# Seven products for eight in a 256-token block of an output projection, and reciprocal roots that start on ScalarE

## The chip, the cores and the metric

The kernel runs on one core of a Trainium2 chip, as one launch. The metric is the device time of that launch in microseconds (us), before and after the change. A core has five engines with queues of their own, each of which works in order: PE (TensorE, the matmuls), DVE (VectorE), ACT (ScalarE), POOL (GpSimd) and SP (SyncE, which here only starts transfers). They wait for one another by semaphores. PE's results go to PSUM, from which DVE and ACT read them; everything else lies in SBUF or, for inputs, outputs and scratch, in DRAM.

## The reference

One decoder layer on 4096 tokens of width 1024, in float32. All three mixers (a gated MLP over chunks, a gated linear recurrence, a forgetting attention) read the same normed and projected input; what they give is concatenated to `y`, and one output projection adds it to `x`. A last norm closes. The part that matters here:

```python
def _rmsnorm(x, g):
    xf = x.astype(jnp.float32)
    y = xf * lax.rsqrt(jnp.mean(xf * xf, axis=-1, keepdims=True) + NORM_EPS)
    return (y * g.astype(jnp.float32)).astype(x.dtype)
...
        y = jnp.concatenate([y_a, y_b, y_c], axis=-1)
        x = x + jnp.einsum('bse,ed->bsd', y, w_out[layer])
    return _rmsnorm(x, final_norm_g)
```

`w_out` is 1024 x 1024, so the last product is 4096 x 1024 x 1024.

## The kernel before

The kernel has three stages one after the other: the input projection with the first two mixers (to about 1620 us), the attention (1651 to 3031), and the output projection (from 3031.3 to the end). Float32 products are made of three PE passes: each operand is split into a high part, rounded to the type that PE multiplies fast (`hi`), and the rest (`lo`), and hi·hi + hi·lo + lo·hi is summed in PSUM. The split of an operand is one ACT copy (the rounding) and one DVE subtraction.

The output projection takes 32 tiles of 128 tokens (`out_tile`), two of which make a block of 256 tokens with index t. For a block, `y_load` brings `y` (transposed) from DRAM scratch in two tiles `yr0` and `yr1`, by five transfers, and `y_split` splits them into `yhi` and `ylo`, in tiles of 128x1024. `w_out` was loaded and split during the attention by `load_wo`, into eight pairs `wo_hi`, `wo_lo` of 128x1024, one for each 128 rows. For a tile, each of the two column halves is one PSUM tile `o` of 24 matmuls (8 row groups times three passes) of 128 x 128 by 128 x 512 (L1588), so 96 matmuls a block. DVE adds the PSUM half to `x` (L1592), ACT squares the sum and adds it up along the row (L1594); then the second half of the generator, run while the next tile multiplies, adds both halves' sums (L1596), takes the reciprocal root in `rsqrt_small` (L99 to L106: a first guess from the bits and three Newton steps, eleven small DVE operations with the two around them), scales the tile with it and with the norm's weights `fgB` (L1600), and writes it out (L1601).

`x` comes into tiles named `x3` (the profile drops the digit: `x`), which rotate over four buffers `qb0` to `qb3` that the attention used for its queries. PE's order is that of the program text (it is scheduled by hand); the order on the other engines is set at build time by the framework's scheduler, and is fixed when the program runs. A pool's buffer is given out in turn: a tile that takes a buffer over waits until the last reader of the tile before has ended, and a load into it until an output transfer from it has landed.

`rsqrt_small` serves other norms too: the one at the start for the first tokens' `x` (names `xr0`, `xr1`), one for the other tokens' (`xr`), and two within the mixers (`gr`, `or`).

## Time and profile before

| what | us |
|---|---|
| three runs, median (lowest to highest) | 3394.76 (3393.18 to 3395.24) |
| the profiled execution | 3389.97 |
| its span | 3388.1 |
| first matmul of the output projection starts | 3031.3 |
| last matmul of the output projection starts | 3379.4 |

The mean clock granted to PE was 0.985 of full speed. Busy times over the whole span: PE 3264.9 us (96%), DVE 2337.5 (69%), ACT 1615.7 (48%), POOL 1383.7 (41%). In the output projection POOL does next to nothing: 3.00 us in 348. In a row of a group or line the columns are the line and engine, operation, tiles (written from read), shape, count, busy us, mean ns of one, and the idle time of that engine ahead of it with what ended it. In a row of a window they are the window, its length, the busy us of PE, weight loads, DVE, ACT and POOL, the granted clock, the DMA share and GB/s.

### The profile page before, as it was taken

The numbers are of one execution on the slowest core, as the hardware profiler recorded it, in microseconds if no ns is written. First come the engines' busy times: TensorE is split into PE (matmuls) and PEld (weight loads), VectorE is DVE, ScalarE is ACT, GpSimd is POOL, SyncE is SP. The second block draws the span as 40 slices with busy tenths as digits, with TensorE's granted clock in tenths as the row PEclk, the third lists the DMA queues.
The fourth block names the chain that finished last, engine by engine and source line by source line (L and its number), as shares of the span: only waits on it lengthen the run. The fifth ranks groups of instructions, "written<-read, shape, count | busy, mean of one in ns | idle before, by whom it ended". The sixth has DMA issues, their size and how long they took to land.

```text
span 3388.1 us, 54808 instructions
## 1 busy us (share of the span) xinstructions
PE 3264.9 (96%) x20314; PEld 2401.5 (71%) x20314; DVE 2337.5 (69%) x4521; ACT 1615.7 (48%) x2979; POOL 1383.7 (41%) x1504
## 2 busy tenths in 40 slices
PE   7999999999999999989899999999999999999999
PEld 7888787978888788777655555555555555558887
DVE  5467745686466845687388888888888888665554
ACT  5435553355434543355255555555555555552221
POOL 2134312342223321344265666666666676660000
PEclk9999999999999999989899999999999999999999
DMA  4432243213342133312550142014201411014443
GB/s 152 138 101 70 70 130 123 94 60 113 114 128 76 51 98 102 104 57 63 123 133 25 35 129 63 26 35 126 66 26 35 116 54 35 27 59 146 148 144 112
DMA packets 204898, 297.06 MB, mean 88 GB/s; under 512 B 19588, under 2 KB 127252, under 8 KB 204630
## 3 DMA queue, kind: packets, MB, share of 16 engines
q1 hardware_dynamic: 204630, 293.56, 28.7%
q8 instruction: 159, 2.61, 0.3%
q14 instruction: 109, 0.89, 0.1%
HBM read 208.83 MB, written 84.43 MB: 87 GB/s over the span
## 4 chain that ended last, share of the span: by engine, by line
PE 53%; DVE 10%; issue 1%; POOL 1%; ACT 1%; DMA 0%; SPq 0%; DVEq 0%; POOLq 0%; ACTq 0%
PE pv L1371 12%; PE o L1588 10%; PE st L1485 7%; PE acc L953 7%; PE sm L149 7%; PE st L1488 6%; DVE mp L162 3%; DVE acc L1354 2%; PE acc L989 2%; PE pl L1311 1%; DVE wlo L249 1%; POOL acc L1354 0%; DVE sm L157 0%; DVE rn L1318 0%; DVE xq L545 0%
## 5 line engine op out<-in xcount | busy, mean ns | idle before, releaser
L1492 ACT ACTIVATE pt<-st,bias 128x512 f32<-128x512 f32 (+3 forms) x1152 | 705.9, 651 | 530.4 <-PE st L1488 431.5
L1354 POOL TENSOR_TENSOR acc<-acc,pt 128x512 f32<-128x512 f32 (+2 forms) x516 | 635.1, 1231 | 316.4 <-PE st L1485 224.4
L162 DVE TENSOR_REDUCE mp<-sm 128x2 f32<-128x1024 f32 (+1 forms) x460 | 536.0, 1192 | 142.9 <-PE sm L149 142.9
L953 PE MATMUL acc<-hhi,whi 128*128 128x512 f32 x1376 | 558.6, 406 | 13.6 <-ACT gu L778 11.1
L953 PE MATMUL acc<-hlo,whi 128*128 128x512 f32 x1376 | 545.3, 396 | 1.3 <-DVE hlo L313 1.3
L953 PE MATMUL acc<-hhi,wlo 128*128 128x512 f32 x1376 | 546.0, 397 | 0.0
L1371 PE MATMUL pv<-pt,v 128*64 128x512 f32 (+3 forms) x2304 | 491.1, 567 | 1.1 <-POOL pt L1497 0.7
L1485 PE MATMUL st<-qa,ka 128*128 128x512 f32 (+2 forms) x1152 | 466.3, 407 | 7.2 <-ACT pt L1492 6.2
L1354 DVE TENSOR_TENSOR acc<-acc,pt 128x512 f32<-128x512 f32 (+2 forms) x516 | 416.2, 807 | 74.8 <-PE pv L1371 34.5
L1488 PE MATMUL st<-qc,kb 68*128 68x512 f32 (+2 forms) x1152 | 441.1, 384 | 3.5 <-DMA qc<-d_m 3.5
L149 PE MATMUL sm<-kb,qb 66*128 66x512 f32 (+2 forms) x1152 | 355.6, 390 | 25.3 <-DVE mp L162 16.1
L1371 PEld LDWEIGHTS pv<-pt,v 128*64 128x64 f32 x2304 | 154.4, 137 | 277.2 <-issue 253.6
L1485 PEld LDWEIGHTS st<-qa,ka 128*128 128x128 f32 x1152 | 219.6, 191 | 179.0 <-issue 96.5
L953 PEld LDWEIGHTS acc<-hhi,whi 128*128 128x128 f32 x1376 | 260.4, 189 | 75.6 <-ACT gu L778 12.5
L249 DVE SCALAR_TENSOR_TENSOR wlo<-wraw,gT,whi 128x256 fp32r<-128x256 f32 (+1 forms) x480 | 255.7, 572 | 75.9 <-ACT whi L248 74.6
L953 PEld LDWEIGHTS acc<-hhi,wlo 128*128 128x128 f32 x1376 | 260.2, 189 | 61.0
L989 PE MATMUL acc<-whi,hhi 128*128 128x256 f32 (+1 forms) x1024 | 295.4, 288 | 7.5 <-ACT FL L996 5.7
L953 PEld LDWEIGHTS acc<-hlo,whi 128*128 128x128 f32 x1376 | 261.0, 190 | 58.0 <-DVE hlo L313 2.3
L989 PE MATMUL acc<-wlo,hhi 128*128 128x256 f32 (+1 forms) x1024 | 289.3, 283 | 0.0
L989 PE MATMUL acc<-whi,hlo 128*128 128x256 f32 (+1 forms) x1024 | 289.1, 282 | 0.0
L149 PEld LDWEIGHTS sm<-kb,qb 66*128 66x128 f32 x1152 | 211.5, 192 | 93.2 <-DVE mp L162 38.2
L1488 PEld LDWEIGHTS st<-qc,kb 68*128 68x128 f32 x1152 | 222.0, 193 | 37.6 <-issue 3.9
(274 smaller groups left out, 4988.4 us busy)
## 6 DMA issues: line engine op xcount, KB each, us to landing
wraw<-in_w_in_dram SPq DMA_DIRECT2D x120, 512.0 KB
x<-in_x_dram SPq DMA_DIRECT2D x88, 512.0 KB
qa<-d_qh SPq DMA_DIRECT2D x64, 256.0 KB
out_dram<-x SPq DMA_DIRECT2D x31, 512.0 KB
kb<-d_kh SPq DMA_DIRECT2D x38, 256.0 KB
d_kh<-chi SPq DMA_DIRECT2D x32, 256.0 KB
d_kl<-clo SPq DMA_DIRECT2D x32, 256.0 KB
d_qh<-chi SPq DMA_DIRECT2D x32, 256.0 KB
```

The lines of the kernel that those rows point to most:

```text
L149: nc.tensor.matmul(ps[:, :n], qb[0:66, h, i * P : (i + 1) * P], kb[0:66, h, :n], start=True, stop=True)
L162: nc.vector.tensor_reduce(dst, ps, axis=AX.X, op=ALU.max)
L249: nc.vector.scalar_tensor_tensor(lo[:, k, :n], raw, g, hi[:, k, :n].bitcast(F32), op0=ALU.mult, op1=ALU.subtract)
L953: nc.tensor.matmul(ps, ww[:, k, cs], hh[:, k, :], start=n == 0, stop=n == 3 * KC - 1)
L989: nc.tensor.matmul(o, hh[:, k, ts_], ww[:, k, :width], start=n == 0, stop=n == 3 * KC - 1)
L1311: nc.tensor.matmul(pl[64 * h : 64 * h + 64, :], ones_v, acc[h], start=True, stop=True)
L1354: ins = eng.tensor_tensor(a[:, q0:], src[:, q0:], pts[i][:, q0:], op=ALU.add)
L1371: mm = nc.tensor.matmul(pv[64 * h : 64 * h + 64, q0:], vt[:, i, 64 * h : 64 * h + 64], group[h][i][:, q0:], start=kb == 0, stop=kb == nkb - 1,
L1485: first = nc.tensor.matmul(st[:, qm:], ka_t[g][:, h, cs], qa_t[u % 2][:, h, qm:], start=True, stop=False)
L1488: nc.tensor.matmul(st[:, qm:], kb_t[g][0:68, h, cs], qc_t[u % 2][:, h, qm:], start=False, stop=True)
L1492: nc.scalar.activation(pt[:, q0:], st[:, q0:], AF.Exp, bias=bias_of[u][:, h, kb : kb + 1])
L1588: nc.tensor.matmul(ps, a[:, k % 4, o : o + P], b[k][:, cs], start=n == 0, stop=n == 3 * KC - 1)
```

## The change

It has two parts.

*The reciprocal roots.* `rsqrt_small` no longer starts from the bits: ACT computes exp(-0.5 · ln(mean + eps)) in two small activations, and DVE does one Newton step in place of three: v, t, t, y, four small operations (L101, L105, L106, L107). Every norm in the kernel uses it.

*The output projection.* The first two blocks (four tiles, `NCL` = 2) go as before. Beside each of these tiles, `combine(k)` loads two row groups of `w_out` once more and makes four combinations of their quarters, each split again (four DVE subtractions, four ACT copies, four DVE splits). The 14 blocks that follow are computed in quarters by the scheme of Strassen in the form with 15 additions: the block's `y` is cut into a11 and a21 (the first and the last 128 tokens of `yr0`, which holds the first half of the sum's length) and a12 and a22 (the same of `yr1`); POOL makes the four sums s1 to s4 of them (L1674), and all seven operands are split (ACT copy L1668, DVE subtraction L1669, in tiles `ya`). `out_block` then runs seven products m0 to m6 of 12 matmuls each (L1716). m1 and m2 lie in the two halves of one PSUM tile `ab`, the others in a ring of three tiles `pr`. DVE adds m0, m1, m2, m4, m5 and m6 to the quarters x11, x12, x21, x22 they belong to (L1722; `x0` and `x1` are the block's two `x3` tiles). ACT copies m0 to `u`, DVE adds m3 to it (L1724), and POOL adds `u` to three quarters (L1726). `norm_out` squares a whole tile of 1024 columns at once, x1 after m5 and x0 after m6, and the final product (L1611) follows. The `x0` tiles go through the buffers `qb0` to `qb3` in turn, the `x1` tiles through the pool named `x`. The load of block 2's `x0` follows, on SP, the output transfer of tile 3, and waits until that has landed.

The diff, cut to what matters:

```diff
--- before
+++ after
+    eps_c = const.tile([P, 1], F32, name="eps_c")
+    nc.gpsimd.memset(eps_c, EPS)
...
         nc.vector.tensor_scalar(v, ssum, scale, EPS, op0=ALU.mult, op1=ALU.add)
-        nc.vector.tensor_scalar(
-            y.bitcast(I32), v.bitcast(I32), -0.5, 1597463007.0, op0=ALU.mult, op1=ALU.add
-        )
-        for _ in range(3):
-            nc.vector.tensor_tensor(t, y, y, op=ALU.mult)
-            nc.vector.scalar_tensor_tensor(t, t, -0.5, v, op0=ALU.mult, op1=ALU.mult)
-            nc.vector.scalar_tensor_tensor(y, t, 1.5, y, op0=ALU.add, op1=ALU.mult)
+        nc.scalar.activation(y, ssum, AF.Ln, scale=scale, bias=eps_c)
+        nc.scalar.activation(y, y, AF.Exp, scale=-0.5)
+        nc.vector.tensor_tensor(t, y, y, op=ALU.mult)
+        nc.vector.scalar_tensor_tensor(t, t, -0.5, v, op0=ALU.mult, op1=ALU.mult)
+        nc.vector.scalar_tensor_tensor(y, t, 1.5, y, op0=ALU.add, op1=ALU.mult)
         return y
...
+        wo = {}
+        KH = KC // 2
...
+        def wo_cost():
+            k = len(wo)
+            return (3, 2) if k >= KH else (5, 4) if k % 2 == 0 else (1, 0)
...
         def load_wo():
-            k = len(wo_hi)
+            k = len(wo)
             raw = big.tile([P, D], F32, tag="big", name="wor")
-            hi = big.tile([P, D], F32R, tag="big", name="woh")
-            lo = big.tile([P, D], F32R, tag="big", name="wol")
             nc.sync.dma_start(raw, wv[:, k, :])
-            nc.scalar.copy(hi, raw)
-            nc.vector.tensor_tensor(lo, raw, hi.bitcast(F32), op=ALU.subtract)
-            wo_hi.append(hi)
-            wo_lo.append(lo)
...
+            for c in range(2):
+                hi, lo = wo[k][c]
+                half = raw[:, c * 512 : c * 512 + 512]
+                nc.scalar.copy(hi, half)
+                nc.vector.tensor_tensor(lo, half, hi.bitcast(F32), op=ALU.subtract)
...
+        NCL = min(2, NSB)
...
+        def x3_load(i, tag):
+            xt = (qp if tag else xp).tile([P, D], F32, tag=tag or "x", name="x3")
+            nc.sync.dma_start(xt, x[0, i * P : (i + 1) * P, :])
+            return xt
+        def norm_out(i, xt):
+            ss = fs.tile([P, 1], F32, tag="ss", name="ss")
+            junk = fs.tile([P, D], BF16, tag="zt", name="junk3", bufs=1)
+            nc.scalar.activation(junk, xt, AF.Square, accum_out=ss)
+            yield
+            rs = rsqrt_small(fs, ss, 1, 1.0 / D, "fr")
+            for cs in (slice(0, 512), slice(512, D)) if i == NT - 1 else (slice(0, D),):
+                nc.vector.scalar_tensor_tensor(xt[:, cs], xt[:, cs], rs, fgB[:, cs], op0=ALU.mult, op1=ALU.mult)
+                nc.sync.dma_start(out[0, i * P : (i + 1) * P, cs], xt[:, cs])
         def out_tile(i):
             t, o = i // 2, (i % 2) * P
-            xt = qp.tile([P, D], F32, tag=f"qb{i % NQB}", name="x3")
-            nc.sync.dma_start(xt, x[0, i * P : (i + 1) * P, :])
-            ss = fs.tile([P, 2], F32, tag="ss", name="ss")
+            xt = x3_load(i, f"qb{i % NQB}")
             for c in range(2):
                 ps = ps_sm.tile([P, 512], F32, tag="sm", name="o")
                 n = 0
-                cs = slice(c * 512, c * 512 + 512)
                 for k in range(KC):
                     hi, lo = yy[t][k // 4]
-                    for a, b in ((hi, wo_hi), (hi, wo_lo), (lo, wo_hi)):
+                    for a, b in ((hi, 0), (hi, 1), (lo, 0)):
                         nc.tensor.matmul(
-                            ps, a[:, k % 4, o : o + P], b[k][:, cs], start=n == 0, stop=n == 3 * KC - 1
+                            ps, a[:, k % 4, o : o + P], wo[k][c][b], start=n == 0, stop=n == 3 * KC - 1
                         )
                         n += 1
+                cs = slice(c * 512, c * 512 + 512)
                 nc.vector.tensor_tensor(xt[:, cs], ps, xt[:, cs], op=ALU.add)
-                junk = pp.tile([P, 512], BF16, tag="p", name="junk3")
-                nc.scalar.activation(junk, xt[:, cs], AF.Square, accum_out=ss[:, c : c + 1])
-            yield
-            nc.vector.tensor_tensor(ss[:, 0:1], ss[:, 0:1], ss[:, 1:2], op=ALU.add)
-            rs = rsqrt_small(fs, ss[:, 0:1], 1, 1.0 / D, "fr")
-            for cs in (slice(0, 512), slice(512, D)) if i == NT - 1 else (slice(0, D),):
-                nc.vector.scalar_tensor_tensor(xt[:, cs], xt[:, cs], rs, fgB[:, cs], op0=ALU.mult, op1=ALU.mult)
-                nc.sync.dma_start(out[0, i * P : (i + 1) * P, cs], xt[:, cs])
+            return norm_out(i, xt)
...
+        def combine(k):
+            raw = [xp.tile([P, D], F32, tag="x", name="wr") for _ in range(2)]
+            for r, kk in zip(raw, (k, k + KH)):
+                nc.sync.dma_start(r, wv[:, kk, :])
...
+            for i, (t, a, b) in enumerate(((t1, b12, b11), (t2, b22, t1), (t3, b22, b12), (t4, b21, t2))):
+                nc.vector.tensor_tensor(t, a, b, op=ALU.subtract)
+                hi, lo = place(4 * k + i)
+                nc.scalar.copy(hi, t)
+                nc.vector.tensor_tensor(lo, t, hi.bitcast(F32), op=ALU.subtract)
+                comb[i][k] = (hi, lo)
+        def a_parts(t):
+            (a11, a21), (a12, a22) = [(r[:, :, 0:P], r[:, :, P:]) for r in yraw[t]]
+            def split(v):
+                pr = big.tile([P, 2, 4, P], F32R, tag="big", name="ya")
+                nc.scalar.copy(pr[:, 0], v)
+                nc.vector.tensor_tensor(pr[:, 1], v, pr[:, 0].bitcast(F32), op=ALU.subtract)
+                parts[t].append(pr)
+            def comb2(a, b, op, tag, n):
+                v = fs.tile([P, 4, P], F32, tag=tag, name="s", bufs=n)
+                nc.gpsimd.tensor_tensor(v, a, b, op=op)
+                return v
+            split(a11)
+            yield
+            s1 = comb2(a21, a22, ALU.add, "rt", 2)
+            split(s1)
+            yield
+            s3 = comb2(a11, a21, ALU.subtract, "rc", 3)
+            split(s3)
+            yield
+            s2 = comb2(s1, a11, ALU.subtract, "rt", 2)
+            split(s2)
+            yield
+            s4 = comb2(a12, s2, ALU.subtract, "rc", 3)
+            split(s4)
+            yield
+            split(a22)
+            yield
+            split(a12)
+        parts, xts = {}, {}
+        def out_block(t):
+            x0, x1 = xts.pop(t)
+            x11, x12, x21, x22 = x0[:, :512], x0[:, 512:], x1[:, :512], x1[:, 512:]
+            ab = ps_sm.tile([P, 2, 512], F32, tag="sm", name="ab")
+            b11 = [wo[k][0] for k in range(KH)]
+            b21 = [wo[k + KH][0] for k in range(KH)]
+            b22 = [wo[k + KH][1] for k in range(KH)]
+            plan = [
+                (b11, [x11]), (comb[0], [x12, x22]), (comb[2], [x21, x22]), (comb[1], []),
+                (b22, [x12]), (comb[3], [x21]), (b21, [x11]),
+            ]
+            for m, (b, adds) in enumerate(plan):
+                pr = parts[t][m]
+                ps = ab[:, m - 1] if m in (1, 2) else ps_st.tile([P, 512], F32, tag="st", name="pr")
+                n = 0
+                for k in range(KH):
+                    for i, w in ((0, b[k][0]), (0, b[k][1]), (1, b[k][0])):
+                        nc.tensor.matmul(ps, pr[:, i, k], w, start=n == 0, stop=n == 3 * KH - 1)
+                        n += 1
+                if m == 0:
+                    u = fs.tile([P, 512], F32, tag="rc", name="u", bufs=3)
+                    nc.scalar.copy(u, ps)
+                for xx in adds:
+                    nc.vector.tensor_tensor(xx, ps, xx, op=ALU.add)
+                if m == 3:
+                    nc.vector.tensor_tensor(u, ps, u, op=ALU.add)
+                    for xx in (x22, x21, x12):
+                        nc.gpsimd.tensor_tensor(xx, xx, u, op=ALU.add)
+                if m == 5:
+                    og.append(norm_out(2 * t + 1, x1))
+                    next(og[-1])
+                yield
+            del parts[t]
+            og.append(norm_out(2 * t, x0))
+            next(og[-1])
         og = []
-        for i in range(NT):
+        for i in range(2 * NCL):
             g = out_tile(i)
             next(g)
             t = i // 2
-            if i % 2 == 0 and t + 1 < NSB:
+            if i % 2 == 0 and t + 1 < NCL:
                 yy[t + 1] = y_split(yraw[t + 1])
-            if i % 2 == 1:
-                del yy[t]
-                if t + 2 < NSB:
-                    yraw[t + 2] = y_load(t + 2)
+            if i % 2 == 1 and t + 2 < NSB:
+                yraw[t + 2] = y_load(t + 2)
+            if NCL < NSB:
+                combine(i)
             tick(og)
             og.append(g)
+            if i == 2 * NCL - 1 and NCL < NSB:
+                parts[NCL] = []
+                drain([a_parts(NCL)])
+                xts[NCL] = [x3_load(2 * NCL, "qb0"), x3_load(2 * NCL + 1, "")]
+        for t in range(NCL, NSB):
+            nxt = []
+            if t + 1 < NSB:
+                parts[t + 1] = []
+                nxt.append(a_parts(t + 1))
+            for m, _ in enumerate(out_block(t)):
+                tick(og)
+                tick(nxt)
+                if m == 1 and t + 1 < NSB:
+                    xts[t + 1] = [x3_load(2 * t + 2, f"qb{(t + 1 - NCL) % NQB}"), x3_load(2 * t + 3, "")]
+                if m == 4 and t + 2 < NSB:
+                    yraw[t + 2] = y_load(t + 2)
         drain(og)
```

How the order of the built program changes, at the two places that matter. On DVE, where one tile (x3_31819, before) ends and the next (x3_31903) begins; `o` is a column half's product:

```order
L106 SCALAR_TENSOR_TENSOR fry_31971<-frt_31972,fry_31971 128x1 [waits DVE_49]
L1600 SCALAR_TENSOR_TENSOR x3_31819<-x3_31819,fry_31971,fgB_29641 128x1024 [waits DVE_49]
L1592 TENSOR_TENSOR x3_31903<-o_31906,x3_31903 128x512 [waits DMAHW6_49,DMAHW5_49,PE_49]
L1564 TENSOR_TENSOR ylo_31883<-yr1_31796,yhi_31882 128x1024 [waits DMAHW2_49,DMAHW1_49,DMAHW3_49,DMAHW0_49,PE_49]
L1592 TENSOR_TENSOR x3_31903<-o_31934,x3_31903 128x512 [waits PE_49]
L1596 TENSOR_TENSOR ss_31905<-ss_31905 128x1 [waits Activation_49]
L99 TENSOR_SCALAR frv_32054<-ss_31905 128x1 [waits DVE_49]
```

On DVE after the change, where block t ends (x3_30118 is its x1, x3_30116 its x0) and block t + 1 begins (x3_30288 and x3_30290; `pr_30411` is its m0, `ab_30410` its m1; ya_30480 and ya_30502 are low parts of its s3 and s2):

```order
L1611 SCALAR_TENSOR_TENSOR x3_30118<-x3_30118,fry_30377,fgB_29444 128x1024 [waits DVE_49]
L101 TENSOR_SCALAR frv_30427<-ss_30407 128x1 [waits Activation_49]
L105 TENSOR_TENSOR frt_30429<-fry_30428 128x1 [waits Activation_49]
L106 SCALAR_TENSOR_TENSOR frt_30429<-frt_30429,frv_30427 128x1 [waits DVE_49]
L107 SCALAR_TENSOR_TENSOR fry_30428<-frt_30429,fry_30428 128x1 [waits DVE_49]
L1611 SCALAR_TENSOR_TENSOR x3_30116<-x3_30116,fry_30428,fgB_29444 128x1024 [waits DVE_49]
L1722 TENSOR_TENSOR x3_30288<-pr_30411,x3_30288 128x512 [waits DMAHW7_49,DMAHW4_49,Activation_49]
L1669 TENSOR_TENSOR ya_30480<-s_30478,ya_30480 128x512 [waits Activation_49]
L1669 TENSOR_TENSOR ya_30502<-s_30500,ya_30502 128x512 [waits PE_49,Activation_49]
L1722 TENSOR_TENSOR x3_30288<-ab_30410,x3_30288 128x512 [waits PE_49]
L1722 TENSOR_TENSOR x3_30290<-ab_30410,x3_30290 128x512
```

Before, the next tile's sum stood behind one final product of the tile before. Now the adds that read m1 stand behind two final products of the block before, with the four small operations of a root between them, the add of m0 and two splits.

On PE, before, where the second column half of a tile begins (o_31822 is the first half's PSUM tile, o_31850 the second's):

```order
L1588 MATMUL o_31822<-wol_29478,yhi_31715 128x512
L1588 MATMUL o_31822<-woh_29477,ylo_31716 128x512
L1588 MATMUL o_31850<-woh_29032,yhi_31711 128x512 [waits DVE_49]
L1588 MATMUL o_31850<-wol_29033,yhi_31711 128x512
L1588 MATMUL o_31850<-woh_29032,ylo_31712 128x512
```

On PE after the change, where m2 begins in the second half of `ab_30410` (th and tl are high and low parts of combined weights; 12 rows of ya_30285 are m1, those of ya_30308 m2):

```order
L1716 MATMUL ab_30410<-tl_29834,ya_30285 128x512
L1716 MATMUL ab_30410<-th_29833,ya_30285 128x512
L1716 MATMUL ab_30410<-th_29552,ya_30308 128x512 [waits DVE_49,Activation_49]
L1716 MATMUL ab_30410<-tl_29553,ya_30308 128x512
L1716 MATMUL ab_30410<-th_29552,ya_30308 128x512
```

Before, a column half waited for the DVE add that had last read its own PSUM buffer, some tiles back. Now the first matmul of m2 waits for a DVE instruction too: it is the second add of m1, `x3_30290<-ab_30410`, the last row of DVE's piece above.

More of the change, by code (lines that the diff above doesn't have):

```diff
@@ L1383, in do_pv @@
                 vslots[0] += 1
-        wo_hi, wo_lo = [], []
+        wo = {}
+        KH = KC // 2
         wv = w_out[0].rearrange("(k p) c -> p k c", p=P)
+        def wo_cost():
+            k = len(wo)
+            return (3, 2) if k >= KH else (5, 4) if k % 2 == 0 else (1, 0)
         def load_wo():
-            k = len(wo_hi)
+            k = len(wo)
             raw = big.tile([P, D], F32, tag="big", name="wor")
-            hi = big.tile([P, D], F32R, tag="big", name="woh")
-            lo = big.tile([P, D], F32R, tag="big", name="wol")
             nc.sync.dma_start(raw, wv[:, k, :])
-            nc.scalar.copy(hi, raw)
-            nc.vector.tensor_tensor(lo, raw, hi.bitcast(F32), op=ALU.subtract)
-            wo_hi.append(hi)
-            wo_lo.append(lo)
+            if k >= KH:
+                new = [big.tile([P, 2, 512], F32R, tag="big", name=n) for n in ("woh", "wol")]
+                wo[k] = [[t[:, c] for t in new] for c in range(2)]
+            elif k % 2 == 0:
+                new = [[big.tile([P, 2, 512], F32R, tag="big", name=n) for n in ("woh", "wol")] for c in range(2)]
+                for i in range(2):
+                    wo_next[k + i] = [[t[:, i] for t in ts] for ts in new]
+            if k < KH:
+                wo[k] = wo_next.pop(k)
+            for c in range(2):
[3 more added lines that the diff above has]
+                nc.vector.tensor_tensor(lo, half, hi.bitcast(F32), op=ALU.subtract)
+        wo_next = {}
         NSLOT, NV, LEAD = 24, 10, 8 * NJ + 24
@@ L1542, in tile_trunk @@
         drain(fin)
-        while len(wo_hi) < KC:
+        while len(wo) < KC:
             load_wo()
+        NCL = min(2, NSB)
         def y_load(t):
@@ L1599, in out_tile @@
-            for cs in (slice(0, 512), slice(512, D)) if i == NT - 1 else (slice(0, D),):
-                nc.vector.scalar_tensor_tensor(xt[:, cs], xt[:, cs], rs, fgB[:, cs], op0=ALU.mult, op1=ALU.mult)
-                nc.sync.dma_start(out[0, i * P : (i + 1) * P, cs], xt[:, cs])
+            return norm_out(i, xt)
+        homes = [(pp, "p", {})] * 13 + [(qp, "v", dict(bufs=10))] * 10
+        homes += [(ac, f"acc{i % 2}", {}) for i in range(4)] + [(fs, "tri", dict(bufs=1))]
+        comb = [{}, {}, {}, {}]
```

17 lines of the change are left out of this document (15 added, 2 removed).

## The prediction

> **What bounds the kernel now.** I read the page's engine line first, then a window over the output projection, then that stage's matmuls, groups and waits, then the end of the timeline, and last what the trace has on prices.
>
> ```profile
> PE 3264.9 (96%) x20314; PEld 2401.5 (71%) x20314; DVE 2337.5 (69%) x4521; ACT 1615.7 (48%) x2979; POOL 1383.7 (41%) x1504
> 3031.00:3379.00 348.00, 348.00 (x1536) 287.88 (x1535) 175.55 (x497) 76.44 (x157) 3.00 (x3) 1.00 0.38 134
> L1588 PE MATMUL o<-woh,yhi x512: 388/389/497, 3031.3 to 3378.9; 128*128 128x512 f32 x171
> L1588 PE MATMUL o<-woh,ylo x512: 388/389/395, 3031.9 to 3379.4; 128*128 128x512 f32 x171
> DVE x L1592 <- PE o L1588: 90.0, 45, 4.7
> DVE ylo L1564 <- PE o L1588: 25.2, 14, 1.8
> ```
>
> TensorE is busy 96% of the span and without a hole in the output stage, at full clock (the 1.00 ahead of the DMA share). The other engines wait for it: VectorE 90.0 us for its sums, and no row there has PE waiting. 1536 matmuls start from 3031.33 to 3379.40, 0.2268 us each; their listed 389 ns overlap. A 128-token tile (48) is 10.89 us, a block of 256 tokens 21.77, the stage from first matmul to the span's end (3388.1) 356.8. Only fewer or later matmuls change this stage.
>
> **The change, part by part.** *Removed.* 14 of 16 blocks issue 84 matmuls instead of 96: 14 × 12 × 0.2268 = 38.1 us, if PE stays the bound. Then a block takes 19.05, each of its seven products (m0 to m6, 12 matmuls) 2.72.
>
> *Added on the path: m2's wait.* Products m1 and m2 are halves of one PSUM tile, `ab`. As built, the first matmul of m2 waits for VectorE's second add that reads m1. That add stands on VectorE behind the previous block's two final products, themselves behind Square, Ln and Exp. So the block is a loop through VectorE, and I price it with these rows:
>
> ```profile
> L1592 DVE TENSOR_TENSOR x<-o,x 128x512 f32<-128x512 f32 x62 | 42.8, 690 | 96.8 <-PE o L1588 96.8
> L1600 DVE SCALAR_TENSOR_TENSOR x<-x,fry,fgB 128x1024 f32<-128x1024 f32 x31 | 39.8, 1285 | 1.1
> L1594 ACT ACTIVATE junk<-x 128x512 bf16<-128x512 f32 x62 | 39.1, 631 | 228.7 <-DVE x L1592 214.5 <-issue 14.2
> L1564 DVE TENSOR_TENSOR ylo<-yr,yhi 128x1024 fp32r<-128x1024 f32 x29 | 35.5, 1225 | 29.6 <-PE o L1588 27.0 <-ACT yhi L1563 2.6
> L104 DVE TENSOR_TENSOR frt<-fry 128x1 f32<-128x1 f32 x93 | 14.8, 159 | 3.2
> L1354 POOL TENSOR_TENSOR acc<-pt x28: 1277/1292/1587, 1673.0 to 2959.7; 128x512 f32<-128x512 f32 x28
> L1354 DVE TENSOR_TENSOR acc<-pt x28: 682/909/1676, 1683.3 to 2966.4; 128x512 f32<-128x512 f32 x28
> L265 ACT ACTIVATE junk<-x x32: 1037/1052/1073, 5.1 to 888.2; 128x1024 bf16<-128x1024 f32 x32
> L560 ACT ACTIVATE dec<-z x16: 192/208/211, 60.8 to 1526.1; 128x4 f32<-128x4 f32 x16
> 3379.40 0.39 PE L1588 MATMUL o<-woh,ylo 128*128 128x512 f32 x1
> 3379.83 0.69 DVE L1592 TENSOR_TENSOR x<-o,x 128x512 f32<-128x512 f32 x1 [4.75 <-PE o L1588]
> 3380.55 0.63 ACT L1594 ACTIVATE junk<-x 128x512 bf16<-128x512 f32 x1 [4.67 <-DVE x L1592]
> 3381.09 0.19 ACT L1594 ACTIVATION_READ_ACCUMULATOR junk<-x 128x1 f32 x1
> 3381.31 0.16 DVE L1596 TENSOR_TENSOR ss<-ss 128x1 f32<-128x1 f32 x1 [0.79 <-ACT junk L1594]
> 3381.50 0.15 DVE L99 TENSOR_SCALAR frv<-ss 128x1 f32<-128x1 f32 x1
> 3383.43 0.16 DVE L106 SCALAR_TENSOR_TENSOR fry<-frt,fry 128x1 f32<-128x1 f32 x1
> 3383.63 1.41 DVE L1600 SCALAR_TENSOR_TENSOR x<-x,fry,fgB 128x512 f32<-128x512 f32 x2
> ```
>
> From these: a sum reaches VectorE 0.2 us after its product's last slot (3379.83 against 3379.40 + 0.2268). A 128x512 VectorE op is 0.69 whether it reads PSUM (L1592) or undisturbed SBUF (682 ns at L1354), a final product 1.285, a small op 0.195 from start to start (11 from 3381.50 to 3383.63). A 512-wide op on POOL is 1.29. A 1024-wide Square until VectorE goes on is 1.05 plus the tail's 0.13: 1.18. Ln and Exp, 0.21 each like L560's 128x4 Exp, plus hand-overs: 0.55. A 512-wide cast is taken as L1594's 0.63.
>
> The loop, with zero at m2's start: m3 ends 5.44; VectorE adds it to `u` until 6.33; POOL's three adds end at 10.25. Behind them, in VectorE's order: add of m4 11.0; low part of a12 11.7; ScalarE casts a11 to 12.35, its low part 13.05; add of m5 13.75; low part of s1 14.45. Square of x1 and its Ln, Exp from 13.8 end at 15.55; two small ops 15.95; add of m6 16.65; one small op, final product of x1 18.15. Square of x0 ran from 16.7, Ln and Exp to 18.45; three small ops 19.05; final product 20.3; then the next block's add of m0 21.0, low parts of s3 and s2 22.4, two adds of m1 23.8. Then m2 starts again: 23.8 us, while PE had work for 19.05 and stood 4.7. DMA waits lie inside this; ScalarE's seven casts lie in the 23.8 too.
>
> *Collisions.* The low parts of a12, a11 and s1 run while POOL makes the next s1 to s4 (10.25 to 15.4). L1354 on VectorE beside a POOL that is 65% busy has a median of 909 ns against 682; L1396, wider, goes from 1211 to 1950:
>
> ```profile
> L1396 DVE TENSOR_TENSOR wol<-wor,woh x8: 1211/1950/2039, 2676.9 to 2995.9; 128x1024 fp32r<-128x1024 f32 x8
> 1700.00:2900.00 1200.00, 1176.91 (x5210) 688.72 (x5206) 1014.65 (x1461) 673.94 (x1122) 776.97 (x842) 0.99 0.24 63
> ```
>
> Three ops at +0 to +0.73, and up to +0.6 on POOL's adds: between 0 and 2.8; I take 3 × 0.23 = 0.7, the row of the same shape.
>
> *The clock.* PE idle for 4.7 us has a price that the trace shows once very plainly:
>
> ```profile
> 3014.57 0.79 PE L1485 MATMUL st<-qa,ka 128*128 128x512 f32 x1 [3.41 <-ACT pt L1492]
> 3005.81:3009.23 3.42, 3.42 (x17) 1.05 (x16) 1.95 (x3) 2.05 (x3) 1.81 (x2) 1.00 0.00 0
> 3009.23:3012.64 3.41, 1.93 (x8) 1.06 (x6) 3.31 (x3) 0.00 (x0) 2.43 (x2) 1.00 0.00 0
> 3012.64:3016.05 3.41, 1.48 (x4) 1.19 (x5) 0.21 (x1) 3.01 (x5) 3.25 (x3) 0.50 0.00 0
> 3016.05:3019.47 3.42, 3.42 (x12) 2.28 (x12) 1.51 (x1) 2.79 (x5) 1.44 (x4) 0.50 0.47 138
> 3019.47:3022.88 3.41, 3.41 (x18) 1.16 (x15) 2.44 (x4) 0.00 (x0) 0.07 (x1) 1.00 0.54 169
> ```
>
> After a hole of 3.41 us the granted clock is 0.50 for two stretches of 3.41 us (column before the DMA share), 4.9 us of them after work resumed; the stretch before had PE busy 1.93 of 3.41. A hole of 4.7 leaves at least one stretch emptier than that wherever it falls. So m2 and m3 begin at half clock for something between 1.6 and 5 us; a mean of 3.3 loses 1.65 us, on the path to `u`, and the hole stays as long. The ends are 0 and 2.5; I take 1.65. The Trainium skill, page "TensorE: Matmul & The Clock Gate", section "What's actually happening", asks for a whole idle window of about 3.4 us for the drop. A hole of 4.7 would hold such a window in about four blocks of ten; by that rule the sum would lose some 14 us of what I charge, near 3440. In the row a window with 1.93 us of work was followed by the drop, so I go by the row.
>
> Cycle: 23.8 + 0.7 + 1.65 = 26.1 us against 21.77 before (ends 23.8 and 29.1).
>
> *Classic tiles, transition, end.* Four tiles stay as before, 43.5; VectorE also makes the combined weights there (8 × 0.69 a tile beside its own work), hidden under 10.89 of PE: 0 to 5, I take 2. The first x of block 2 takes over a buffer of tile 3, whose output must land first:
>
> ```profile
> 3199.98 0.34 SPq L1601 DMA_DIRECT2D out_dram<-x  x1
> 3203.07 0.33 SPq L1579 DMA_DIRECT2D x<-in_x_dram  x1
> ```
>
> That landing takes 3.1 (SP's x load stands behind it), and I give the load the same: tile 3's final product about 6 after its last matmul, +3.1, +3.1, then the add of m0 and two adds of m1: m2 of block 2 starts 14.3 after tile 3 (bounds 8 and 17). Twelve cycles follow; the one into block 15 has no low parts to make for a next block, 21.0 + 1.65; from its m2 to the end the same order without them gives a last final product at 18.4 plus 3.1 landing, 21.5 + 1.65. Stage: 43.5 + 2 + 14.3 + 12 × 26.1 + 22.65 + 23.15 = 418.8, against 356.8: **+62**.
>
> *The roots.* Each loses 7 small VectorE ops and gains Ln and Exp on ScalarE. PE waits for one only at the start:
>
> ```profile
> PE xtp L306 <- DVE x L291: 8.1, 2, 6.3
> PE xtp L306 <- DVE xr1t L105: 6.2, 1, 6.2
> PE xtp L306 <- DVE xr1t L104: 2.6, 1, 2.6
> L1070 ACT ACT_TABLE_LOAD  x1: 1283/1283/1283, 0.8 to 0.8; - x1
> ```
>
> Per root 7 × 0.195 − 0.55 = 0.8 less in those four waits: −3 (0 to −5). Elsewhere PE's work covers them: 0, between −4 and +3. One table load serves all functions so far, the Exp among them; if Ln with Exp needed another, each switch costs at least 1.28. I take none, and −1 for attention, where the weights' load is cut in halves (±3).
>
> Together +62 − 4 = +58 on the profiled execution: 3389.97 (span 3388.1) to 3448. The median shown is 4.8 higher: **3453 us**.
>
> **The rivals.**
> - *VectorE keeps up (faster).* If its queue reaches m1's adds as soon as m1 ends, PE waits only 0.2 + 2 × 0.69 a block: cycle 20.6. 43.5 + 14.3 + 13 × 20.6 + 21.5 = 347, less 4: 3382. For it: VectorE is busy 175.55 of 348 us now, and its own work in a block of the new loop is only about 15 us (16 ops of 0.69, two of 1.285, eight of 0.195). Against it: the order, in which POOL's 3.9 us and two Squares are waited out in line. It decides at a cycle under 21.7; there the sum equals before.
> - *PE alone bounds.* No wait at m2 at all: −38 − 4 and a few us for the transition: 3355. Against it: the wait in the built program.
> - *The loop without collisions and without the clock's drop.* Cycle 23.8: 43.5 + 14.3 + 12 × 23.8 + 21 + 21.5 = 386, +29 − 4: 3420.
> - *Everything collides and the drop lasts.* Cycle 29.1: 36 more than my sum, 3489.
>
> **How the numbers follow.** Two measured times of this kernel differ with certainty from about 0.2% (7 us) on. The loop with collisions and clock drop, 3425 to 3485: 0.60. The loop without them, 3402 to 3425: 0.15. VectorE in time: 0.10. PE alone: 0.07. Above 3485: 0.04. Between, 3388 to 3402: 0.04. Faster therefore 0.17, same 0.04, slower 0.79. The range 3378 to 3485 leaves out PE alone, the lower half of VectorE in time, and the top: 0.16. The likeliest case's own range is 3425 to 3485.
>
> **What the profile after would show.** PE waiting at L1716 for VectorE's L1722 in some 14 places, 4 to 6 us each; a clock of about 0.9 in the stage from 3075 on; one wait of about 9 us at block 2; VectorE's add of m4 waiting for POOL's L1726; block to block 24 to 28 us. If PE stays above 95% busy there, the loop is wrong and the time is below 3390. If the holes are there with the clock at 1.00, the drop was mis-sized; if VectorE's low parts stay at 0.69, the collisions.

## The result, and the profile after

The kernel became slower: 3477.07 us (median of four runs, 3475.47 to 3480.25) against 3393.97 for the kernel before on the same chip, a ratio of 1.0251 with an interval of 1.0239 to 1.0264. The forecast was 3453. The profiled execution took 3477.75, with a span of 3476.0 against 3388.1, so 87.9 us more. (One slip in the description above: the buffers that `x3` rotates over are three, `qb0` to `qb2`. No number rests on it.)

First the page's engine line and a window over the output stage, from block 2's surroundings to the end:

```profile
PE 3271.8 (94%) x20146; PEld 2394.6 (69%) x20146; DVE 2373.6 (68%) x4144; ACT 1679.3 (48%) x3173; POOL 1524.8 (44%) x1603
3085.00:3476.00 391.00, 305.25 (x1181) 244.87 (x1179) 215.14 (x369) 106.58 (x223) 138.78 (x94) 0.87 0.29 104
```

PE, busy for all of 348 us before, is now busy 305 of 391 at a mean clock of 0.87. No engine is full: VectorE is busy 55% of that window. The waits of that stage (us in total, times, longest) say where PE stands:

```profile
PE ab L1716 <- DVE x L1722: 77.7, 14, 11.7
DVE x L1722 <- POOL x L1726: 52.0, 14, 3.9
POOL x L1726 <- DVE u L1724: 238.3, 14, 20.8
```

The timeline shows the first matmul of m2 in several blocks (start, duration, and in the bracket the idle time of PE ahead of it and what ended it):

```profile
3103.20 0.77 PE L1716 MATMUL ab<-th,ya 128*128 128x512 f32 x1 [11.68 <-DVE x L1722]
...
3266.85 0.77 PE L1716 MATMUL ab<-th,ya 128*128 128x512 f32 x1 [5.38 <-DVE x L1722]
3294.15 0.77 PE L1716 MATMUL ab<-th,ya 128*128 128x512 f32 x1 [5.38 <-DVE x L1722]
...
3430.65 0.76 PE L1716 MATMUL ab<-th,ya 128*128 128x512 f32 x1 [5.38 <-DVE x L1722]
3454.03 0.47 PE L1716 MATMUL ab<-th,ya 128*128 128x512 f32 x1 [1.47 <-DVE x L1722]
```

There are 14 waits of PE, one a block, and the twelve cycles from 3103.20 to 3430.65 take 27.29 us each on average; before, a block took 21.77. In each of the twelve PE stands 5.37 or 5.38 us at the same place.

The same cycle cut along the stretches in which the clock is set (busy PE, weight loads, VectorE, ScalarE, POOL, then the clock), the counterpart of the five rows shown of before:

```profile
3258.76:3262.17 3.41, 2.71 (x12) 1.90 (x11) 2.97 (x8) 2.02 (x5) 0.48 (x1) 1.00 0.00 0
3262.17:3265.58 3.41, 0.00 (x0) 0.00 (x0) 3.34 (x7) 1.66 (x4) 0.00 (x0) 0.99 0.69 268
3265.58:3269.00 3.42, 2.15 (x5) 1.81 (x6) 1.73 (x3) 0.00 (x0) 0.00 (x0) 0.50 1.00 309
3269.00:3272.41 3.41, 3.41 (x9) 2.67 (x9) 0.06 (x1) 0.00 (x0) 0.00 (x0) 0.51 0.48 191
3272.41:3275.82 3.41, 3.41 (x16) 2.76 (x16) 1.86 (x3) 0.62 (x1) 0.00 (x0) 1.00 0.49 154
```

An empty stretch, then two at half clock: m2 begins at 3266.85, and the following 5.5 us of work, to about 3272.4, run at half speed. And the loop itself, VectorE and POOL from m2 of one block to m2 of the next:

```profile
3275.19 0.69 DVE L1724 TENSOR_TENSOR u<-pr,u 128x512 f32<-128x512 f32 x1 [1.55 <-PE pr L1716]
3275.96 4.22 POOL L1726 TENSOR_TENSOR x<-x,u 128x512 f32<-128x512 f32 x3 [16.72 <-DVE u L1724]
3280.22 0.69 DVE L1722 TENSOR_TENSOR x<-pr,x 128x512 f32<-128x512 f32 x1 [3.68 <-POOL x L1726]
...
3284.80 1.74 POOL L1674 TENSOR_TENSOR s<-yr,s 128x512 f32<-128x512 f32 x1
3286.67 0.69 DVE L1722 TENSOR_TENSOR x<-pr,x 128x512 f32<-128x512 f32 x1
3287.46 1.28 DVE L1611 SCALAR_TENSOR_TENSOR x<-x,fry,fgB 128x1024 f32<-128x1024 f32 x1
3289.72 1.28 DVE L1611 SCALAR_TENSOR_TENSOR x<-x,fry,fgB 128x1024 f32<-128x1024 f32 x1
3290.92 0.68 DVE L1722 TENSOR_TENSOR x<-pr,x 128x512 f32<-128x512 f32 x1
3292.72 1.28 DVE L1722 TENSOR_TENSOR x<-ab,x 128x512 f32<-128x512 f32 x2
```

Read downwards: the add to `u`, POOL's three adds, the add of m4 that waited 3.68 for them, POOL's last sum for the next block, the add of m6, two final products, the add of m0, and the two adds of m1, 0.15 us after which m2 starts. It is the order that the prediction walked through.

Term by term, in the profiled execution (a "stage" time ends at the span's end):

| term | forecast | measured | difference |
|---|---|---|---|
| up to the output's first matmul, against before | −4 | +6.4 (3037.7 against 3031.3) | +10.4 |
| four classic tiles | 45.5 | 48.2 (3037.7 to 3085.9) | +2.7 |
| tile 3's end to block 2's m2 | 14.3 | 17.3 | +3.0 |
| twelve cycles | 12 × 26.1 | 12 × 27.29 | +14.3 |
| the cycle into block 15, and the end | 22.65 + 23.15 | 23.38 + 21.97 | −0.5 |

Together +29.9 on the forecast span of 3446, which gives 3476.

### The profile page after: what moved, and what is told of

Read it like the earlier page. It is cut to its first block, busy times and chain, and to the rows that moved or that the text cites. A ratio compares the mean times of both kernels' runs of the same rounds, so it can differ in the third digit from the quotient of the medians.

```text
span 3476.0 us, 54457 instructions
## 1 busy us (share of the span) xinstructions
PE 3271.8 (94%) x20146; PEld 2394.6 (69%) x20146; DVE 2373.6 (68%) x4144; ACT 1679.3 (48%) x3173; POOL 1524.8 (44%) x1603
## 5 line engine op out<-in xcount | busy, mean ns | idle before, releaser
L150 PE MATMUL sm<-kb,qb 66*128 66x512 f32 (+2 forms) x1152 | 355.7, 390 | 24.9 <-DVE mp L163 16.9
```

Of the source, the lines that this page charges most:

```text
L150: nc.tensor.matmul(ps[:, :n], qb[0:66, h, i * P : (i + 1) * P], kb[0:66, h, :n], start=True, stop=True)
```

## Experiments

All ratios are to the kernel before, run in turn with it on the same chip. "After" in a diff means that the changed kernel was edited, "before" the first one.

**Is it the shared PSUM tile? (`split`)** After, with m1 and m2 in two PSUM tiles of their own:

```diff
-            ab = ps_sm.tile([P, 2, 512], F32, tag="sm", name="ab")
+            ab = [ps_sm.tile([P, 512], F32, tag="sm", name=f"ab{i}") for i in range(2)]
-                ps = ab[:, m - 1] if m in (1, 2) else ps_st.tile([P, 512], F32, tag="st", name="pr")
+                ps = ab[m - 1] if m in (1, 2) else ps_st.tile([P, 512], F32, tag="st", name="pr")
```

> The products m1 and m2 get a PSUM tile each; nothing else is changed. Theory (VectorE's queue is the loop, and PE is tied into it by the shared tile ab): PE runs ahead of VectorE, the loop then closes only from one add to u to the next, about 21 us (in the changed kernel the add to u starts at 3275.2 and the two adds of m1 of the next block end at about 3294.1: 18.9, then 0.7 + 1.3 for a low part and two adds), instead of 27.3; 14 x 6.3 less: 3477 - 88 = 3389, between 3375 and 3410. Rival (VectorE, ScalarE and POOL simply have too much to do in a block, and PE would wait at another place): within 10 us of 3477.

3379.98 us (3378.42 to 3381.26), ratio 0.9963 (0.9950 to 0.9976): 97 us gone with an edit of two lines, and the kernel is now a little faster than before. A window over some ten blocks of this kernel, its waits, and the place in the timeline where PE waits now, in two blocks:

```profile
3150.00:3350.00 200.00, 190.38 (x828) 154.18 (x826) 147.54 (x257) 75.67 (x158) 98.68 (x68) 1.00 0.41 148
```

```profile
PE pr L1716 <- DVE x L1722: 13.5, 12, 1.8
```

```profile
3207.90 0.47 PE L1716 MATMUL pr<-woh,ya 128*128 128x512 f32 x1 [1.08 <-DVE x L1722]
3228.34 0.47 PE L1716 MATMUL pr<-woh,ya 128*128 128x512 f32 x1 [1.09 <-DVE x L1722]
```

The wait at `ab` is gone, the clock is 1.00, a cycle is 20.43 (3228.34 − 3207.90). What is left is a wait of 1.1 us at a `pr` tile, against the 19.05 that 84 matmuls take. So the tie of PE to VectorE's queue through `ab` cost 27.29 − 20.43 = 6.9 us a block. VectorE's order is the same as in after: the two adds of m1 still stand behind two final products of the block before, the add of m0 and two splits, and m2 no longer waits for them. That the wait came from the shared tile, and not from the data, is shown.

**How much of it is the clock? (`fill`)** After, with 22 matmuls that do no part of the computation ahead of m2, so that PE does not stand idle:

```diff
+                if m == 2:
+                    fill = ps_st.tile([P, 512], F32, tag="st", name="pr")
+                    for _ in range(22 if t < NSB - 1 else 0):
+                        nc.tensor.matmul(fill, parts[t][3][:, 0, 0], comb[1][0][0], start=True, stop=True)
-                ps = ab[:, m - 1] if m in (1, 2) else ps_st.tile([P, 512], F32, tag="st", name="pr")
+                ps = ab[:, m - 1] if m in (1, 2) else fill if m == 3 else ps_st.tile([P, 512], F32, tag="st", name="pr")
```

> Ahead of m2, PE does 22 matmuls more (5.0 us) into the PSUM tile that m3 then overwrites, so that the hole of 5.4 us is filled and its clock stays up; all blocks but the last. Theory (the hole also costs the half clock after it, which lies on the loop): the cycle falls from 27.3 to about 24.8, 13 x 2.5: 3477 - 33 = 3444, between 3435 and 3455, with a granted clock near 1.00. Rival (the clock is only a sign of the hole; PE has slack there): 3477, or more.

3443.62 us (3440.26 to 3444.82), ratio 1.0151 (1.0136 to 1.0166), as expected. The window over the stage, and one of the starts of m2:

```profile
3085.00:3440.00 355.00, 336.42 (x1453) 273.07 (x1451) 212.02 (x366) 104.63 (x219) 136.91 (x92) 0.99 0.32 113
```

```profile
3250.33 0.50 PE L1720 MATMUL ab<-th,ya 128*128 128x512 f32 x1 [0.31 <-DVE x L1726]
```

22 more matmuls a block made the kernel 33 us faster. With the clock at 0.99 the cycle is 24.66 us (3225.66 to 3299.64 are three), so VectorE's loop alone, collisions included, is 24.66 and the half clock added 27.29 − 24.66 = 2.6 a block.

**Each part alone (`roots`, `allclassic`).** Before, with the new reciprocal roots only (the first part of the change); and after, with `NCL` such that all 16 blocks go the classic way, which leaves the roots and the loading of `w_out` in halves:

```diff
--- roots, from before
-        for _ in range(3):
...
+        nc.scalar.activation(y, ssum, AF.Ln, scale=scale, bias=eps_c)
+        nc.scalar.activation(y, y, AF.Exp, scale=-0.5)
...
--- allclassic, from after
-        NCL = min(2, NSB)
+        NCL = NSB
```

> The kernel before, with the new reciprocal roots only. In the trace of the changed kernel the attention's first product starts 10.5 us earlier (1637.0 against 1647.5). Theory: that is the roots': 3391 - 10 = 3381, attention and output stage unchanged. Rival (the prediction's reading: only the four waits at the start shrink, by 3): 3388.

> The changed kernel with all 16 blocks the classic way: new roots, and the weights loaded in halves, but no seven products and no combined weights. In the changed kernel's trace the attention is 16.9 us longer than before. Theory (the halved loads in the attention cost that): 3391 - 10 + 17 = 3398. Rival (that loss belongs to something else of the scheme, or is scatter of the attention): as roots, 3381.

`roots`: 3382.03 us (3377.85 to 3386.46), ratio 0.9978 (0.9969 to 0.9987). The roots give 8.6 us, not 3. `allclassic`: 3393.99 (3392.37 to 3396.40), ratio 1.0012 (1.0002 to 1.0021): by the medians the halved weights take 12.0 of it back, by the two profiled spans (3392.0 and 3383.7) 8.3. The attention's score matmuls by their line, their first and last start at the end of the columns, in `roots` and in `allclassic`:

```profile
L1485 PE MATMUL st<-qa,ka x1152: 278/396/795, 1640.5 to 3020.8; 128*128 128x512 f32 x160, 128*128 128x256 f32 x32
```

```profile
L1503 PE MATMUL st<-qa,ka x1152: 278/396/796, 1640.7 to 3028.3; 128*128 128x512 f32 x160, 128*128 128x256 f32 x32
```

The same row has 1647.5 to 3024.4 in before (the description above put the start at 1651) and 1637.0 to 3030.6 in after. So with the new roots the attention starts 6.8 to 10.5 us earlier, and from first to last it takes 1376.9 us in before, 1380.3 in `roots`, 1387.6 in `allclassic` and 1393.6 in after. Where the halves cost, the timeline of `allclassic` shows (ScalarE's copies of two weight halves, then the two longest holes of PE in the attention's end):

```profile
2969.60 1.14 ACT L1413 CAST woh<-wor 128x512 fp32r<-128x512 f32 x2 [7.02 <-DVE wol L1414]
2971.38 0.79 PE L1503 MATMUL st<-qa,ka 128*128 128x512 f32 x1 [5.88 <-ACT pt L1510]
3018.45 0.80 PE L1503 MATMUL st<-qa,ka 128*128 128x512 f32 x1 [4.74 <-ACT pt L1510]
```

A copy waits 7.02 us for VectorE's subtraction of an earlier half, the attention's exponentials (`pt`) stand behind the copy on ScalarE, and PE waits 5.88 us for them. The hole of 4.74 stands behind a copy of `yhi` for the output stage, not of the weights. `roots`, with whole rows as before, has in this stretch the second of these holes alone, and shorter:

```profile
3010.61 0.80 PE L1485 MATMUL st<-qa,ka 128*128 128x512 f32 x1 [3.41 <-ACT pt L1492]
```

The difference, 5.88 and 4.74 less 3.41, is 7.2 us of the 8 to 12; the rest was not settled. That the attention of after takes 6 us longer still than that of `allclassic` needs no cause in the seven products: after and eight other kernels that differ from it in the output stage alone take from 1387.6 us (`split`) to 1393.8 (`splitx12`) for it, in one profiled execution each.

**The weights in another order (`splitwo`).** `split`, with the rows of `w_out` loaded in the order 4 to 7, 0 to 3, to take that copy out of the way:

```diff
-            k = len(wo)
+            k = (len(wo) + KH) % KC
```

> As split, and the eight row groups of the weights are loaded in the order 4 to 7, 0 to 3 (those whose column halves share a tile first), so that no raw tile waits with a half unsplit. Theory: in allclassic one ACT copy of the weights stood 7.0 us for a VectorE split, behind it the attention's exponentials, and PE waited 5.9 and 4.7 us where roots has one wait of 3.4; with the other order the attention is as in roots: 3380 - 11 = 3369. Rival (the loss of 12 us comes from halves as such, more and shorter operations): 3380.

3381.48 us (3374.48 to 3390.42), ratio 0.9971 (0.9962 to 0.9981): the same as `split`. The wait only moved:

```profile
2995.52 0.62 ACT L1413 CAST woh<-wor 128x512 fp32r<-128x512 f32 x1 [6.56 <-DVE wol L1414]
2996.78 0.79 PE L1503 MATMUL st<-qa,ka 128*128 128x512 f32 x1 [5.43 <-ACT pt L1510]
```

**Work moved off the loop: three misses.** First `u`'s three adds from POOL to VectorE, in after (`udve`):

```diff
-                        nc.gpsimd.tensor_tensor(xx, xx, u, op=ALU.add)
+                        nc.vector.tensor_tensor(xx, xx, u, op=ALU.add)
```

> The changed kernel, but the three adds of u are VectorE's (3 x 0.69 = 2.1 us) instead of POOL's (4.2 us). Theory: these lie on the loop; without the clock's loss the cycle goes from 24.75 to 22.6; the hole stays above 3 us and so the half clock after it, of 0 to 2.6 us. If the loop locks to the clock's stretches of 3.413 us, as 27.31 = 8 of them suggests, it comes out at 7 of them, 23.9: 3477 - 14 x 3.4 = 3429; unlocked between 3411 and 3446. Rival (POOL's adds are off the path): 3477 or, with VectorE's added work, above.

3479.48 us (3476.6 to 3479.7), ratio 1.0262 (1.0248 to 1.0276): nothing gained. The three adds on VectorE, and what POOL did meanwhile:

```profile
3249.59 1.45 POOL L1674 TENSOR_TENSOR s<-yr,yr 128x512 f32<-128x512 f32 x1 [20.73 <-DMA yr<-d_yc]
3249.81 5.17 DVE L1726 TENSOR_TENSOR x<-x,u 128x512 f32<-128x512 f32 x3
3251.11 1.62 POOL L1674 TENSOR_TENSOR s<-s,yr 128x512 f32<-128x512 f32 x1
```

They took 5.17 us, not 3 × 0.69 = 2.07, while POOL, now free, made the next block's sums. The work left POOL, but its time did not leave the loop: PE's hole ahead of m2 is 6.15 to 6.18 us in nine of the twelve cycles and 5.11 or 5.12 in three, against 5.38 in after.

Second, the final products put on VectorE behind the next block's adds of m1 instead of ahead of them: in after (`later`) and in `split` (`splitlater`).

```diff
+            for _ in range(late):
+                yield
+            with tc.issue_after(last[0]) if late else nullcontext():
...
+                    add = nc.vector.tensor_tensor(xx, ps, xx, op=ALU.add)
+                if m == 2:
+                    last[0] = add.ins
...
+                    og.append(norm_out(2 * t + 1, x1, 4))
...
+            og.append(norm_out(2 * t, x0, 2))
```

> Both roots and final products of a block are put, on VectorE, behind the second add of m2 of the next block; the tile ab stays shared. Theory: m1's adds then no longer stand behind Square, Ln, Exp and the final products; m2 waits only for m1's own two adds, cycle 20.7 (PE 19.05 + 0.2 + 2 x 0.69) and up to 1.7 more where the hole of 1.6 still drops the clock: 14 x 6.6 to 14 x 4.9 less: 3385 to 3408. Rival (the engines' work sets the cycle, its order does not): within 10 us of 3477.

> Both: a PSUM tile each for m1 and m2, and the final products behind m2's adds of the next block. Theory: PE bounds the block, 19.05 to 20 us: 14 x 8.25 to 14 x 7.3 less than 3477: 3361 to 3375, faster than before. Rival (work of VectorE and POOL with their collisions, about 15 + 9 us in a block that must share SBUF, is the bound): above 3430.

`later`: 3466.37 us (3465.75 to 3468.31), ratio 1.0219 (1.0202 to 1.0236), 11 us better than after where about 80 were expected. `splitlater`: 3396.02 (3392.82 to 3400.61), ratio 1.0016 (1.0007 to 1.0026), 16 worse than `split`. In `later`, two of the clock's stretches (the clock stands ahead of the last two columns), and from the timeline m2's start and the moved operations:

```profile
3255.06:3258.48 3.42, 0.58 (x3) 0.16 (x1) 3.06 (x6) 1.88 (x4) 0.00 (x0) 1.00 0.46 152
3258.48:3261.89 3.41, 2.63 (x6) 2.15 (x7) 0.63 (x2) 0.00 (x0) 0.00 (x0) 0.50 0.01 2
```

```profile
3259.26 0.77 PE L1721 MATMUL ab<-th,ya 128*128 128x512 f32 x1 [3.62 <-DVE x L1727]
3266.61 2.48 DVE L1616 SCALAR_TENSOR_TENSOR x<-x,fry,fgB 128x1024 f32<-128x1024 f32 x2
3269.00 0.68 DVE L1731 TENSOR_TENSOR u<-pr,u 128x512 f32<-128x512 f32 x1
3271.90 4.23 POOL L1733 TENSOR_TENSOR x<-x,u 128x512 f32<-128x512 f32 x3
```

The hole at m2 did shrink, to 3.6 us, but by the clock's records half clock still came with eleven of the twelve holes of 3.3 to 3.8 us. The final products, 2.48 us, now stand ahead of the add to `u`, which starts 9.74 us after m2 instead of 8.34; and POOL took two of the next block's sums ahead of its three adds, which start 2.9 after `u`'s add instead of 0.8. What was taken from one half of the loop was put into the other. In `splitlater` the two products stand ahead of the add to `u` too; its 16 us were not taken apart further.

Third, in `split`, the final products behind the add to `u` (`splitu`):

```diff
-                    nc.vector.tensor_tensor(u, ps, u, op=ALU.add)
+                    last[0] = nc.vector.tensor_tensor(u, ps, u, op=ALU.add).ins
...
+                    og.append(norm_out(2 * t + 1, x1, 5))
...
+            og.append(norm_out(2 * t, x0, 3))
```

> A PSUM tile each for m1 and m2 as in split; both roots and final products of a block stand, on VectorE, directly behind the next block's add of m3 to u, where VectorE waits 3.7 us for POOL's three adds in split. Theory (VectorE's queue is still the loop in split, 20.43 us a block, and 3.7 of it are that wait): the loop falls below PE's 19.05, PE bounds at 19.05 to 19.5: 14 x 0.9 to 14 x 1.4 less than 3380: 3360 to 3367. Rival (in later and splitlater it was the delay of output, x and y transfers on SP that cost, and it costs here too): 3385 or more.

3395.78 us (3389.76 to 3399.24), ratio 1.0016 (1.0007 to 1.0024), 16 worse than `split` again. Here the products run while POOL adds, which looked like free time. A window over the same 200 us as in `split`, and the timeline:

```profile
3150.00:3350.00 200.00, 184.93 (x782) 149.56 (x783) 179.72 (x242) 71.91 (x149) 111.64 (x67) 0.97 0.44 151
```

```profile
3229.42 4.39 POOL L1731 TENSOR_TENSOR x<-x,u 128x512 f32<-128x512 f32 x3 [9.57 <-DVE u L1729]
3229.44 1.28 DVE L105 TENSOR_TENSOR frt<-fry 128x1 f32<-128x1 f32 x1
3232.61 2.28 DVE L1616 SCALAR_TENSOR_TENSOR x<-x,fry,fgB 128x1024 f32<-128x1024 f32 x1
```

VectorE is busy 179.72 us of 200 against 147.54 in `split`, with fewer operations (242 against 257): a final product takes 2.28 beside POOL's adds instead of 1.285, and an operation on 128x1, one number in each partition, 1.28 instead of 0.16.

**POOL's order (`x12`, `splitx12`, `splitx12wo`).** The quarter that the next VectorE add needs (m4 is added to x12) made first instead of last, in after, in `split`, and in `splitwo`:

```diff
-                    for xx in (x22, x21, x12):
+                    for xx in (x12, x21, x22):
```

> The changed kernel with POOL's three adds of u in the order x12, x21, x22 instead of x22, x21, x12: VectorE's add of m4 needs only the first. Theory: 2.8 us of the wait leave the loop, some 0.8 come back as collisions of the low parts with POOL's other adds: from 24.75 to about 22.7 without the clock's loss. Locked to the clock's stretches: 23.9, 3477 - 14 x 3.4 = 3429; not locked 3411 to 3446. Rival (as in udve, what VectorE does beside POOL takes as much longer as it starts earlier): 3470 or more.

> As x12 on split. Theory: the loop of 20.43 falls by about 2, below PE's 19.05; PE bounds at 19.05 to 19.4: 14 x 1.0 to 14 x 1.4 less than 3380: 3360 to 3366. Rival (taking turns eats it, as in splitu and udve): 3378 to 3385.

> splitwo and splitx12 together. Theory: both gains add: 3380 - 11 - 17 = 3352. Rival: only the one of the weights' order, 3369.

`x12`: 3477.2 us (3476.35 to 3483.15), ratio 1.0257 (1.0242 to 1.0272), unchanged. `splitx12`: 3378.28 (3375.15 to 3382.6), ratio 0.9960 (0.9948 to 0.9972), not to be told from `split`. `splitx12wo`: 3380.8 (3377.78 to 3386.74), ratio 0.9969 (0.9958 to 0.9980). In `x12` the add of m4 indeed no longer waits for POOL (PE's m4 is what it waits for), and yet, in the timeline:

```profile
3277.00 0.69 DVE L1722 TENSOR_TENSOR x<-pr,x 128x512 f32<-128x512 f32 x1 [1.47 <-PE pr L1716]
...
3284.38 1.29 POOL L1674 TENSOR_TENSOR s<-yr,s 128x512 f32<-128x512 f32 x1
3284.47 1.22 DVE L106 SCALAR_TENSOR_TENSOR frt<-frt,frv 128x1 f32<-128x1 f32 x1
3285.62 0.68 DVE L1722 TENSOR_TENSOR x<-pr,x 128x512 f32<-128x512 f32 x1
```

The 128x1 operation takes 1.22 and ends as POOL's last sum ends, and the add of m6 follows it. POOL's seven operations a block (three adds, four sums) take 10.7 us from the first's start (3274.95) to the last's end in `x12`, and 10.6 in after; the add of m6 comes 10.7 us after that first start in both (3285.62 here, 3286.67 against 3275.96 in after). So, as far as these two traces show, it is not the three adds alone that the loop waits out there, but the block's whole run of POOL work; a kernel without the four sums was not tried. In `splitx12` VectorE is busy 162.58 us of the 200 from 3150 to 3350, against 147.54 in `split`, with 259 operations against 257: what it no longer waits, its operations take longer.

## Why the prediction was right, and where it was off

*The mechanism: right.* It forecast a wait of m2 for VectorE's adds of m1 because both lie in `ab`, in some 14 places of 4 to 6 us, one of about 9 at block 2, blocks of 24 to 28 us, a clock of about 0.9. The trace has 14 waits at L1716 for L1722, twelve of 5.38, one of 11.68 at block 2 and one of 1.47 at the last block, a cycle of 27.29 and a clock of 0.87; `split` took the cause away, and the cost with it.

*The loop, 23.8 + 0.7: right in sum, in part by luck.* 24.66 in `fill`; 27.29 less the clock's 2.70 is 24.6 in after. Laid against the forecast's marks from m2's start, with those 2.70 us taken off, POOL's three adds end at 10.63 (forecast 10.25), the add of m6 at 17.81 (16.65) and the adds of m1 at 24.45 (23.8). Up to the add of m6 the loop is 1.16 behind the marks, of which 0.7 had been allowed for as collisions; from there to the adds of m1 it takes 6.64 where the marks have 7.15. So the first part, collisions included, was sized about 0.5 too low and the rest as much too high: the sum is right because the two cancel. The row behind the collisions (909 against 682 ns) was a mild case: in `udve`, `splitu` and `x12` such operations went to between 1.8 and eight times their length.

*The clock, 1.65: mis-sized, beyond its stated end of 2.5.* It lost 2.70 a block: `u`'s add starts 8.34 after m2 instead of 5.64. I had averaged over where the hole falls between the stretches, for a hole of 4.7. But the records of half and full clock add up to the cycle, 6.83 + 20.48 = 27.31, eight stretches of 3.413, in all twelve cycles: the hole does not fall anywhere, it falls in the same place each time. That is 12 × 1.05 = 13 of the 30 us missed. A reason can be worked out: the half clock ends at a set time, so a block that starts later in its stretch loses less and one that starts earlier loses more, and both are drawn back to the grid (half of 3272.41 − 3266.85 is 2.78, near the 2.70). No run was made for it alone, but `x12` bears it out. Its first m2 starts are 3103.77, 3130.18, 3157.03, 3184.09 and 3211.29, with the same hole of 5.32 or 5.31 ahead of each but the first: the intervals fall short of 27.31 by 0.90, 0.46, 0.25 and 0.11, about half as much each time, and the later ones are 27.2 to 27.3. In `udve` the starts lie 26.34 to 27.94 apart, but its clock has the same twelve cycles of 6.83 and 20.48. So the grid can hide a small gain in the loop: a block that starts earlier loses more clock. It did not hide one in `x12`: the hole, which shows the loop without the clock, is 5.32 there against 5.38, so the loop is shorter by no more than 0.06.

The Trainium skill, page "TensorE: Matmul & The Clock Gate", section "What's actually happening", asks for a whole idle window. After's trace agrees (0.00 busy from 3262.17 to 3265.58); `later` does not: there PE was busy 0.58 us in the stretch from 3255.06, and the drop followed. The forecast by that rule, near 3440, would have been further off.

*Attention, −1 ± 3: wrong.* This step failed in its size and sign: +12.0 by `allclassic` against `roots` (8.3 by their profiled spans), and in the profiled execution of after 16.9 (its output's first matmul is 6.4 later than before's though its attention starts 10.5 earlier). I had taken the halves as the same work cut differently, and not asked what is queued behind each copy on ScalarE. The exponentials are, and a copy that waits for VectorE holds them.

*The roots, −3: too small.* −8.6 alone, outside the 0 to −5 that I gave the start, though within it and the −4 that I allowed elsewhere together. Every traced kernel with the new roots starts the attention earlier than before's 1647.5, at 1637.0 to 1642.2. The four waits at the start that I counted are not the whole of it: PE's waits within the projections changed in several places, some up and some down. The time at half clock ahead of the attention is 44.4 us in `roots` against 51.2 in before, but it lies between 41.0 and 58.0 in the kernels with the new roots, so no part of the 8.6 can be put down to it. No single wait explains 8.6; this is not settled. The second table load that I put at nothing did not come: after has the one, of 1.283 us, too.

*Classic tiles +2 and transition 14.3: low*, the tiles within their bound of 5 (+4.7), the transition just beyond its bound of 17 (17.3). PE stood once for 2.71 us in the tiles (VectorE's combined weights ahead of a sum), and then ran at half clock. At block 2, tile 3's final product came 8.5 us after its last matmul, not 6, behind the low parts of block 2's operands, and the add of m0 started 3.8 us after the load was issued, not 3.1:

```profile
3073.31 0.50 PE L1623 MATMUL o<-woh,yhi 128*128 128x512 f32 x1 [2.71 <-DVE x L1628]
...
3093.16 1.28 DVE L1611 SCALAR_TENSOR_TENSOR x<-x,fry,fgB 128x1024 f32<-128x1024 f32 x1
3097.40 0.33 SPq L1599 DMA_DIRECT2D x<-in_x_dram  x1
3101.17 0.69 DVE L1722 TENSOR_TENSOR x<-pr,x 128x512 f32<-128x512 f32 x1 [4.92 <-DMA x<-in_x_dram]
```

*The 4.8 us added for the median* did not show: after's median lies 0.7 below its profiled execution. That it made up for a part of the misses is luck.

*The rivals.* VectorE in time, at a cycle of 20.6 and 3382, has the numbers of `split`, 20.43 and 3380, but not its mechanism: in `split` VectorE still reaches m1's adds behind the two final products, and PE waits 1.1 us at a `pr` tile and not at m2. It was the shared tile that decided it, not the speed of VectorE.
